# Seven block products in three of eight pairs of channel tiles, and SwiGLU transposes issued ten steps later

## The chip, the core and the metric

The kernel runs on one core of a Trainium2 chip, all by itself. The metric is the device time of one execution in microseconds (us). TensorE (PE) multiplies matrices, VectorE (DVE) and ScalarE (ACT) work element by element, SyncE (SP) issues the transfers (DMAs) that bring weights from the chip's memory into the core's. Every engine works through its own list of instructions in order; semaphores make one wait for another.

## What is computed

A decoder layer for 256 tokens of width 2048 in float32: a norm, one input projection, eight heads of differential attention and eight heads of gated DeltaNet, an output projection, and then the part that the change touches, a norm and a SwiGLU feed-forward block with 5632 hidden channels:

```python
    u = rmsnorm(h, ffn_norm_w[l])
    h = h + (jax.nn.silu(u @ w_gate[l]) * (u @ w_up[l])) @ w_down[l]
```

## The kernel before

Each weight element in float32 is used as the sum of two shorter numbers: `split` (lines 263 to 274) lets ScalarE round a raw weight tile to `hi` (L272) and VectorE take the rest, `lo = raw - hi` (L273). TensorE then computes three products for each block (hi by hi, hi by lo, lo by hi).

The feed-forward block works on chunks of 512 hidden channels; chunk 0 is done by `stream`, chunks 1 to 10 by `chunk` (L1369). In a chunk the 16 channel tiles of `u` (128 channels each) are taken as eight pairs q = 0 to 7, and for each pair a gate weight tile and an up weight tile of 128 x 1024 (512 KB) are loaded. An ordinary pair takes 2 x 2 blocks of tokens and channels for two outputs, 8 block products or 24 matmuls of 512 columns. In the pairs listed in `SEVEN` the same is done with seven block products (Strassen's scheme in Winograd's form), 21 matmuls. For that the weights are combined too: VectorE makes `t` (L290, L291: u1-g1 and u2-u1) and `s` (L296, L297: u2-t1 and g2-s1) from the raw gate tile g and up tile u, and g, half of u, t and s are each split. So an ordinary pair has two weight forms, and a pair of seven has four, called g, u, t and s.

The weights go through rings of buffers. Raw tiles have 4 buffers (`WR`): a load is issued when the tile four places before it has been read for the last time, an ordinary tile by L273, the u and g of a pair of seven by L296 and L297. `hi` and `lo` have 6 buffers: a form's split waits until TensorE is done with the form six places before.

A chunk gathers in four banks x0 to x3 of the matmuls' memory, gate in x0 and x1, up in x2 and x3, and what the seven products share in four other banks, y0 to y3. There are eight banks in all, and two rings of four that change roles from chunk to chunk: the y banks of one chunk are the x banks of the next. After the last pair of seven, `mid_task` (L1337) copies y0 (ScalarE, L1343) and adds up y1 to y3 (VectorE, L1345 to L1348), which frees these banks. After the gate half of pair 7, `end_task` (L1352) adds x0, x1 (L1357), applies SiLU, adds x2, x3 (L1362), multiplies (L1364), waits some steps and goes on in `to_hT` (L1272): TensorE transposes the 128 x 512 result in four pieces (L1277), ScalarE and VectorE copy it out as two parts (L1292, L1293). The transposes use two banks of the x ring of their chunk, which the next chunk needs as its y banks.

What sets the order: the tasks are Python generators, and `tasks.step()` is called after each block product (three matmuls). `yield 2` means that the task goes on two steps later. ScalarE and SyncE keep the order in which the code is written; TensorE and VectorE are ordered by a scheduler of the framework. The profile's names are `aux` and `mm` for the two rings of banks, `gact` for the tiles of `mid_task` and `end_task`, `raw`, `hi`, `lo`, `t` and `s` for the weights, `uh`, `ul`, `sh`, `sl` for the stationary operands.

Of the kernel before, what the change touches and what calls it, by code (L numbers as in the profile page):

```python
# [8 lines left out]
F32 = mybir.dt.float32  # L9
F32R = mybir.dt.float32r  # L10
# [5 lines left out]
P = 128  # L16
D = 2048
KT = D // P
META = 16
SEQ = 256  # L20
T = META + SEQ
FFN = 5632
H = 8
# [8 lines left out]
WR, WS = 4, 4  # L32
WS2 = 2
WHOLE = 8
SEVEN = (2, 5)
PER_STEP = 2
SLOT = 4
WARM = 14
# [127 lines left out]
def layer(tc, xT, aw, x, w_in, w_ba, w_out, w_gate, w_up, w_down, cmask, dist, par, out):  # L166
# [3 lines left out]
    def pool(name, bufs=1, space=None):  # L170
        cm = tc.tile_pool(name=name, bufs=bufs, **({"space": space} if space else {}))
        return cm, cm.__enter__()
# [7 lines left out]
    cm_const, const = pool("const")  # L180
# [6 lines left out]
    cm_work, wk = pool("work")  # L187
# [15 lines left out]
    def act(out_, in_, func, **kw):  # L203

        act_table("silu_and_others" if func == AF.Silu else "natural_log_exp_and_others")
        S.activation(out_, in_, func, **kw)

    def mark(k, n=1):
        done[k] = done.get(k, 0) + n

    def at_least(k, n):
        return lambda: done.get(k, 0) >= n
# [20 lines left out]
    def w_tile(wv, q, c):  # L233
        return wv[:, 2 * q:2 * q + 2, 512 * c:512 * (c + 1)], 2, 512
# [5 lines left out]
    for c in range(1, NCH):  # L240
        for q in range(KT // 2):
            i = len(order)
            order += [w_tile(wv, q, c) for wv in (wg_v, wu_v)]
            forms += [("w", i), ("w", i + 1)] if q not in SEVEN else [("g", i), ("u", i), ("t", i), ("s", i)]
    i = len(order)
# [95 lines left out]
    def mk(n):  # L341
        return cmsk[:, CMI[n] - 1, :]
# [15 lines left out]
    def small(n):  # L358
        smalls[0] += 1
        return const.tile([P, 17], F32, tag="small", bufs=6, name=f"small{smalls[0]}")[:, 0:n]  # L360
# [33 lines left out]
            square((k - 6) // 2)  # L394


    rbc = const.tile([P, T], F32, name="rbc")

    def input_rms():

# [151 lines left out]


    qkv = {n: None for n in "qkv"}
    blk64 = const.tile([P, P], F32R, name="blk64r")
    V.tensor_copy(blk64, mk("blk64"))
    tri_s = const.tile([P, P], F32R, name="tri_sr")
    V.tensor_copy(tri_s, mk("tri_s"))
    cwv = pr("conv_w").rearrange("p (c j) -> p c j", j=4)

# [33 lines left out]
    c2 = const.tile([P, 17], F32, name="c2")  # L594
    rq = const.tile([P, 16], F32, name="rq")
    rq2 = const.tile([P, 16], F32, name="rq2")
    kP = const.tile([P, H, META], F32, name="kP")
    kPf = kP.rearrange("p h t -> p (h t)")

    ktm = {}  # L600

    def sums(which, g, n, dst, keep_it=False):

        ps = yield from aux.get(4, P)
        for i in range(4):
            PE.transpose(ps[:, i, :], qkv[which][:, 4 * g + i, META + P * n:META + P * (n + 1)], ident)
        yield 1
        junk = yield from r1.get(P)
        for i in range(4):
            c = 8 * n + 4 * g + i  # L610
            S.activation(junk, ps[:, i, :], AF.Square, accum_out=dst[:, c:c + 1])
        r1.free()
        if keep_it:
            ktm[g] = yield from r2.get(4, P)
            V.tensor_copy(ktm[g], ps)
        aux.free()

    def k_scalars():
        yield at_least("gates", 1)
        ssk = const.tile([P, 17], F32, name="ssk")  # L620
        for g in range(2):
            yield at_least(f"k{g}", 4)
            yield 3
            for n in range(2):
                yield from sums("k", g, n, ssk, n == 0)
        G.tensor_copy(kP, qkv["k"][:, :, 0:META])
        yield 2
        ps = yield from aux.get(P)
        PE.transpose(ps, kPf, ident)
        yield 1  # L630
        ktm["m"] = const.tile([P, P], F32, name="ktm_m")
        S.activation(ktm["m"], ps, AF.Square, accum_out=ssk[:, 16:17])
        S.copy(ktm["m"], ps)
        aux.free()
        yield 1
        rk, a = small(17), small(17)
        rsqrt_fine(rk, ssk, 1.0, a)
        V.tensor_tensor(ksq, a, rk, ALU.mult)
        V.tensor_tensor(c1, rk, rk, ALU.mult)
        V.tensor_tensor(c1, c1, gb, ALU.mult)  # L640
        V.tensor_tensor(c2, c1, e_rem, ALU.mult)
        mark("c1")
# [709 lines left out]
    def end_task(c, b, x, t):  # L1352
        ring = rings[c % 2]
        yield at_least(f"mid{c}", 1)
        g_, h_ = t[2 * b], t[2 * b + 1]
        r_ = rr[:, b:b + 1]
        V.tensor_tensor(g_, x[b], g_, ALU.add)  # L1357
        ring.free()
        act(g_, g_, AF.Silu, scale=r_)
        yield at_least(f"up{c}", 1)  # L1360
        yield 1
        V.tensor_tensor(h_, x[2 + b], h_, ALU.add)  # L1362
        ring.free()
        V.scalar_tensor_tensor(h_, h_, r_, g_, ALU.mult, ALU.mult)  # L1364
        fpool[1].free()
        yield 2
        yield from to_hT(c, b, h_)

    def chunk(c):  # L1369
# [3 lines left out]
        y, t = [], []  # L1373
        n = KT // 2 - len(SEVEN)
        left = {("x", i): 3 * (2 * n + (len(SEVEN) if i < 3 else 0)) for i in range(4)}
        left.update({("y", i): 3 * len(SEVEN) for i in range(4)})
        todo = dict(left)
# [6 lines left out]
        for q in range(KT // 2):  # L1384
            k = 2 * q
            if q not in SEVEN:
                for col in range(2):
# [16 lines left out]
            for part in plan:  # L1404
                hi, lo = next_w()
                for bank, a, i in part:
                    product(bank, a, (hi[:, i], lo[:, i]))
                    tasks.step()
            if q == SEVEN[-1]:
                tasks.spawn(mid_task(c, y, t), urgent=True)  # L1410
# [146 lines left out]
```

## Time and profile before

| | |
|---|---|
| time, median of 3 runs | 1244.05 us (1243.71 to 1245.04) |
| profiled execution, its own time | 1242.6 us |
| its span, first to last instruction | 1240.8 us |
| TensorE busy | 1228.4 us, 99% |
| VectorE busy | 865.0 us, 70% |
| ScalarE busy | 652.2 us, 53% |
| DMA queue of SyncE | 226.78 MB, 56.6% of 16 engines' span |

Matmuls are pipelined, and the view shows each of them with its latency, 0.39 us, while the next starts 0.23 us after it; a busy TensorE is therefore read by the distance between starts. Inside the span the feed-forward chunks 1 to 10 lie between 558 and 995 us, and the down projection from there to the end. 1.8 us of the profiled execution lie outside its span.

### The profile page before, as it was taken

What the parts mean: (1) busy time and instruction counts of PE and PEld (TensorE: products, weight loads), DVE (VectorE), ACT (ScalarE), POOL (GpSimd) and SP (SyncE); (2) the same over time, 40 slices, a digit from 0 to 9 for tenths busy, and PEclk for the clock granted to TensorE, in tenths of its full rate; (3) what the DMA queues carried; (4) which work ended last, traced back from release to release, by engine and by line L of the source; (5) the groups of instructions that cost most, each with busy time, mean ns of one, the idle gap of its engine ahead of it and who ended that gap; (6) DMA issues with size and microseconds to landing.
All of it is one profiled execution on the core that took longest, in us unless ns stands there. A gap on an engine that the chain in (4) does not pass through costs nothing.

```text
span 1240.8 us, 19041 instructions
## 1 busy us (share of the span) xinstructions
PE 1228.4 (99%) x7388; PEld 1072.9 (86%) x7388; DVE 865.0 (70%) x1357; ACT 652.2 (53%) x1021; POOL 6.0 (0%) x14
## 2 busy tenths in 40 slices
PE   9999999999999999999999999999999999999998
PEld 7999999999999888888888888888888878888887
DVE  7989965686677655667887887788787764444442
ACT  7675465375676654555555555455555553433331
POOL 0000000000000000000000000000000000000000
PEclk9999999999999999999999999999999999999999
DMA  8466553345544555675566656456565675656561
GB/s 292 125 199 194 166 171 120 107 136 153 154 143 147 204 187 183 234 235 163 188 202 200 194 183 219 159 195 207 190 195 190 208 259 195 207 198 206 193 215 52
DMA packets 151003, 228.53 MB, mean 184 GB/s; under 512 B 11640, under 2 KB 72576, under 8 KB 150144
## 3 DMA queue, kind: packets, MB, share of 16 engines
q1 hardware_dynamic: 150368, 226.78, 56.6%
q8 instruction: 58, 0.95, 0.3%
q10 hardware_dynamic: 544, 0.52, 0.1%
q14 instruction: 33, 0.27, 0.1%
HBM read 221.83 MB, written 5.45 MB: 183 GB/s over the span
## 4 chain that ended last, share of the span: by engine, by line
PE 77%; DVE 12%; DMA 4%; ACT 4%; issue 2%; SPq 0%; ACTq 0%; DVEq 0%
PE mm L1152 22%; PE mm L1199 19%; PE aux L1382 10%; PE mm L1382 9%; PE aux L1199 9%; DVE lo L273 6%; ACT hi L272 3%; DMA raw<-in_w_gate_dram 2%; DMA raw<-in_w_up_dram 1%; DVE gact L1357 1%; DVE gact L1362 1%; PE aux L1100 1%; DVE gact L1364 1%; PE aux L1277 1%; PE aux L1055 1%
## 5 line engine op out<-in xcount | busy, mean ns | idle before, releaser
L273 DVE TENSOR_TENSOR lo<-raw,hi 128x1024 fp32r<-128x1024 f32 (+1 forms) x412 | 484.2, 1186 | 291.9 <-ACT hi L272 288.4
L272 ACT CAST hi<-raw 128x1024 fp32r<-128x1024 f32 (+1 forms) x412 | 417.6, 1022 | 428.7 <-PE mm L1199 114.0
L1152 PE MATMUL mm<-xh,hi 128*128 128x272 f32 (+2 forms) x896 | 258.3, 289 | 0.0
L1152 PE MATMUL mm<-xl,hi 128*128 128x272 f32 (+2 forms) x896 | 255.7, 286 | 0.6 <-DVE xl L384 0.6
L1152 PE MATMUL mm<-xh,lo 128*128 128x272 f32 (+2 forms) x896 | 254.9, 285 | 0.8 <-DVE lo L273 0.8
L1152 PEld LDWEIGHTS mm<-xh,hi 128*128 128x128 f32 x896 | 168.7, 189 | 2.1 <-issue 1.5
L1152 PEld LDWEIGHTS mm<-xl,hi 128*128 128x128 f32 x896 | 168.5, 188 | 1.8 <-DVE xl L384 1.5
L1152 PEld LDWEIGHTS mm<-xh,lo 128*128 128x128 f32 x896 | 168.2, 188 | 1.1 <-DVE lo L273 1.0
L1382 PE MATMUL aux<-hi,uh 128*128 128x512 f32 x280 | 109.4, 391 | 0.0
L1382 PE MATMUL mm<-hi,uh 128*128 128x512 f32 x280 | 109.4, 391 | 0.0
L1382 PE MATMUL aux<-hi,ul 128*128 128x512 f32 x280 | 109.3, 390 | 0.0
L1382 PE MATMUL mm<-hi,ul 128*128 128x512 f32 x280 | 109.0, 389 | 0.0
L1382 PE MATMUL aux<-lo,uh 128*128 128x512 f32 x280 | 108.9, 389 | 0.0
L1382 PE MATMUL mm<-lo,uh 128*128 128x512 f32 x280 | 108.9, 389 | 0.0
L1199 PE MATMUL aux<-hi,hT 128*128 128x512 f32 x256 | 79.7, 390 | 0.0
L1199 PE MATMUL mm<-hi,hT 128*128 128x512 f32 x256 | 79.2, 389 | 0.0
L1382 PEld LDWEIGHTS mm<-hi,ul 128*128 128x128 f32 x280 | 52.6, 188 | 11.1
L1382 PEld LDWEIGHTS aux<-hi,ul 128*128 128x128 f32 x280 | 52.6, 188 | 10.8
L1382 PEld LDWEIGHTS aux<-lo,uh 128*128 128x128 f32 x280 | 52.6, 188 | 10.8
L1382 PEld LDWEIGHTS mm<-lo,uh 128*128 128x128 f32 x280 | 52.6, 188 | 10.8
L1382 PEld LDWEIGHTS aux<-hi,uh 128*128 128x128 f32 x280 | 52.6, 188 | 10.8
L1382 PEld LDWEIGHTS mm<-hi,uh 128*128 128x128 f32 x280 | 52.6, 188 | 10.7
(395 smaller groups left out, 1753.0 us busy)
## 6 DMA issues: line engine op xcount, KB each, us to landing
raw<-in_w_in_dram SPq DMA_DIRECT2D x111, 512.0 KB, 3.6
raw<-in_w_gate_dram SPq DMA_DIRECT2D x88, 512.0 KB, 4.2
raw<-in_w_up_dram SPq DMA_DIRECT2D x88, 512.0 KB, 4.5
raw<-in_w_down_dram SPq DMA_DIRECT2D x88, 512.0 KB, 4.4
raw<-in_w_out_dram SPq DMA_DIRECT2D x32, 512.0 KB, 4.1
x1n<-x1d SPq DMA_DIRECT2D x2, 1024.0 KB, 7.7
xr<-in_xT_dram SPq DMA_DIRECT2D x7, 272.0 KB, 5.6
out_dram<-x1n SPq DMA_DIRECT2D x6, 256.0 KB, 5.6
```

Source lines behind the costliest of these rows:

```text
L272: S.copy(hi[:, js], raw[:, js])
L273: V.tensor_tensor(lo[:, js], raw[:, js], hi[:, js], ALU.subtract)
L1055: PE.matmul(pss[m][:, cut[n]], q[ms, P * n:P * (n + 1)], k[ms, 0:NK[n]], start=True, stop=True)
L1100: PE.matmul(po[:, n, :], l, r, start=(j == 0), stop=(j == 1 + n))
L1152: PE.matmul(acc[c][:, 0:n], a[:, k, cs], b[:, kt, t0:T], start=(kt == 0 and i == 0), stop=(kt == KT - 1 and i == 2))
L1199: PE.matmul(acc[b], l, r[:, i % 2, :], start=(first and i == 0 and j == 0), stop=(last and i == len(kts) - 1 and j == 2))
L1277: PE.transpose(pst[:, j, :], h_[:, P * j:P * (j + 1)], ident)
L1357: V.tensor_tensor(g_, x[b], g_, ALU.add)
L1362: V.tensor_tensor(h_, x[2 + b], h_, ALU.add)
L1364: V.scalar_tensor_tensor(h_, h_, r_, g_, ALU.mult, ALU.mult)
L1382: PE.matmul((x if bank[0] == "x" else y)[bank[1]], l, r, start=first, stop=todo[bank] == 0)
```

## The change

`SEVEN` becomes (2, 4, 6): three pairs of seven in a chunk in place of two, and the last of them is pair 6 in place of 5, so that `mid_task` is spawned one pair later. In `end_task` ten steps, in place of two, lie between L1364 and the transposes. Five small tiles move from a pool that lives to the end to one that is closed before the feed-forward block, which makes room for the side operands of the third pair.

```diff
-SEVEN = (2, 5)
+SEVEN = (2, 4, 6)
...
-    rbc = const.tile([P, T], F32, name="rbc")
+    rbc = wk.tile([P, T], F32, name="rbc")
...
         ring.free()
         V.scalar_tensor_tensor(h_, h_, r_, g_, ALU.mult, ALU.mult)
         fpool[1].free()
-        yield 2
+        yield 10
         yield from to_hT(c, b, h_)
```

The tiles `blk64r`, `tri_sr`, `kP` and `ktm_m` move like `rbc`. L-numbers of the changed kernel are the same, since no line is added.

VectorE from the last pair of seven on, before (pairs 5 to 7; raw_8987 and raw_8975 are u and g of pair 5):

```order
L290 TENSOR_TENSOR t_9014<-raw_8987,raw_8975 128x512
L291 TENSOR_TENSOR t_9014<-raw_8987 128x512
L273 TENSOR_TENSOR lo_9018<-raw_8987,hi_9017 128x512
L296 TENSOR_TENSOR s_9033<-raw_8987,t_9014 128x512
L297 TENSOR_TENSOR s_9033<-raw_8975,s_9033 128x512
L273 TENSOR_TENSOR lo_9037<-t_9014,hi_9036 128x1024
L273 TENSOR_TENSOR lo_9057<-s_9033,hi_9056 128x1024
L273 TENSOR_TENSOR lo_9073<-raw_8996,hi_9072 128x1024
```

VectorE in the same place now, from the end of pair 4 to the end of pair 6 (raw_9119 and raw_9091 are u and g of pair 6, raw_8983 is g of pair 4):

```order
L297 TENSOR_TENSOR s_9082<-raw_8983,s_9082 128x512
L273 TENSOR_TENSOR lo_9100<-s_9082,hi_9099 128x1024
L273 TENSOR_TENSOR lo_9116<-raw_9054,hi_9115 128x1024
L290 TENSOR_TENSOR t_9152<-raw_9119,raw_9091 128x512
L273 TENSOR_TENSOR lo_9134<-raw_9089,hi_9133 128x1024
L273 TENSOR_TENSOR lo_9146<-raw_9091,hi_9145 128x1024
L291 TENSOR_TENSOR t_9152<-raw_9119 128x512
L273 TENSOR_TENSOR lo_9156<-raw_9119,hi_9155 128x512
L296 TENSOR_TENSOR s_9165<-raw_9119,t_9152 128x512
L273 TENSOR_TENSOR lo_9169<-t_9152,hi_9168 128x1024
L297 TENSOR_TENSOR s_9165<-raw_9091,s_9165 128x512
L273 TENSOR_TENSOR lo_9183<-s_9165,hi_9182 128x1024
```

The first instruction on the new up tile (L290) now stands ahead of two splits of tiles that were loaded before it, and the split of s stands directly behind L297, with no other split between them.

VectorE from `mid_task` on, before (the `lo` rows are the splits of pairs 1 and 2 of the next chunk; x banks here are aux, y banks mm):

```order
L1345 TENSOR_TENSOR gact_9145<-mm_8968,gact_9144 128x512
L273 TENSOR_TENSOR lo_9163<-raw_9115,hi_9162 128x1024
L1346 TENSOR_TENSOR gact_9146<-mm_8969,gact_9145 128x512
L1347 TENSOR_TENSOR gact_9147<-mm_8970,gact_9146 128x512
L1348 TENSOR_TENSOR gact_9145<-mm_8970,gact_9145 128x512
L273 TENSOR_TENSOR lo_9181<-raw_9127,hi_9180 128x1024
L1357 TENSOR_TENSOR gact_9144<-aux_8868,gact_9144 128x512
L1357 TENSOR_TENSOR gact_9146<-aux_8869,gact_9146 128x512
L273 TENSOR_TENSOR lo_9199<-raw_9139,hi_9198 128x1024
```

VectorE from `mid_task` on, now (lo_9262 is the last split of pair 1 of the next chunk, lo_9289 the first of its pair 2):

```order
L273 TENSOR_TENSOR lo_9262<-raw_9232,hi_9261 128x1024
L1345 TENSOR_TENSOR gact_9271<-mm_9047,gact_9270 128x512
L273 TENSOR_TENSOR lo_9289<-raw_9241,hi_9288 128x1024
L1346 TENSOR_TENSOR gact_9272<-mm_9048,gact_9271 128x512
L1357 TENSOR_TENSOR gact_9270<-aux_8947,gact_9270 128x512
L1347 TENSOR_TENSOR gact_9273<-mm_9049,gact_9272 128x512
L1348 TENSOR_TENSOR gact_9271<-mm_9049,gact_9271 128x512
L1357 TENSOR_TENSOR gact_9272<-aux_8948,gact_9272 128x512
```

`mid_task` now stands behind all splits of pairs 0 and 1 of the next chunk and around the first split of its pair 2; before, the two splits of pair 1 stood in and behind it.

TensorE at the transposes, before (gact_8795 and gact_8797 are the two results of the chunk before; hi_8785 and lo_8786 are the up tile of pair 0):

```order
L1382 MATMUL aux_8871<-lo_8786,uh 128x512
L1277 MATMUL mm_8895<-ident,gact_8795 128x128 x4
L1382 MATMUL aux_8871<-hi_8785,ul 128x512
L1277 MATMUL mm_8900<-ident,gact_8797 128x128 x4
L1382 MATMUL aux_8870<-hi_8785,uh 128x512
```

TensorE at the transposes, now (hi_8888 and hi_8900 are the gate and the up tile of pair 1):

```order
L1382 MATMUL aux_8948<-lo_8889,uh 128x512
L1382 MATMUL aux_8948<-hi_8888,ul 128x512
L1277 MATMUL mm_9013<-ident,gact_8910 128x128 x4
L1277 MATMUL mm_9018<-ident,gact_8912 128x128 x4
L1382 MATMUL aux_8949<-hi_8900,uh 128x512
```

The transposes move from the middle of pair 0 to the middle of pair 1 (in every other chunk, where the rings have changed roles, to three matmuls before its end).

## Rows read from the trace of the kernel before

**Rows 1.** The page: busy time of each engine over the whole span (part 1), and the chain that ended last, its shares by engine (part 4).

```profile
PE 1228.4 (99%) x7388; PEld 1072.9 (86%) x7388; DVE 865.0 (70%) x1357; ACT 652.2 (53%) x1021; POOL 6.0 (0%) x14
...
PE 77%; DVE 12%; DMA 4%; ACT 4%; issue 2%; SPq 0%; ACTq 0%; DVEq 0%
```

**Rows 2.** The chain of waits in order of time, in the feed-forward part: start us, us, what. Each of the three 6.84 us pieces is the first stretch of matmuls behind the transposes of a chunk: of the second chunk, of the third, and of the tenth.

```profile
607.93 6.84 PE mm L1382 x30
...
618.85 11.56 PE mm L1382 x51
...
651.51 6.84 PE aux L1382 x30
...
956.66 6.84 PE mm L1382 x30
```

**Rows 3.** Busy time by stretch, one chunk each: stretch, its us, then us (and count) of PE, PEld, DVE, ACT, POOL, then the granted TensorE clock (1.00 is the upper level, 2.4 GHz), the DMA share and GB/s.

```profile
607.90:651.50 43.60, 43.31 (x196) 35.64 (x195) 34.97 (x41) 23.00 (x25) 0.00 (x0) 1.00 0.59 193
```

**Rows 4.** TensorE in order of time at the start of the third chunk: start us, us, engine, line, operation, tiles, shape, and in brackets the idle time before it and what ended it. The transposes are the rows of L1277.

```profile
649.51 0.39 PE L1382 MATMUL aux<-lo,uh 128*128 128x512 f32 x1
650.18 0.66 PE L1277 MATMUL mm<-ident,gact 128*128 128x128 f32 x4 [0.28 <-DVE gact L1364]
650.60 0.48 PE L1382 MATMUL aux<-hi,ul 128*128 128x512 f32 x1
650.91 0.60 PE L1277 MATMUL mm<-ident,gact 128*128 128x128 f32 x4
651.27 0.48 PE L1382 MATMUL aux<-hi,uh 128*128 128x512 f32 x1
651.58 0.39 PE L1382 MATMUL aux<-lo,uh 128*128 128x512 f32 x1
```

**Rows 5.** The same view behind the last chunk (its transposes stand between matmuls of the down projection).

```profile
998.35 0.66 PE L1277 MATMUL mm<-ident,gact 128*128 128x128 f32 x4 [0.84 <-DVE gact L1364]
...
1000.15 0.66 PE L1277 MATMUL mm<-ident,gact 128*128 128x128 f32 x4 [0.45 <-DVE gact L1364]
```

**Rows 6.** VectorE in order of time around the start of the third chunk (columns as in rows 4; "x2" is two instructions merged).

```profile
642.33 0.68 DVE L1348 TENSOR_TENSOR gact<-aux,gact 128x512 f32<-128x512 f32 x1
642.92 1.21 DVE L273 TENSOR_TENSOR lo<-raw,hi 128x1024 fp32r<-128x1024 f32 x1
644.06 1.28 DVE L1357 TENSOR_TENSOR gact<-mm,gact 128x512 f32<-128x512 f32 x2
...
646.39 0.69 DVE L290 TENSOR_TENSOR t<-raw,raw 128x512 f32<-128x512 f32 x1
...
647.59 0.68 DVE L273 TENSOR_TENSOR lo<-raw,hi 128x512 fp32r<-128x512 f32 x1
648.19 1.28 DVE L1362 TENSOR_TENSOR gact<-mm,gact 128x512 f32<-128x512 f32 x2
649.39 1.40 DVE L1364 SCALAR_TENSOR_TENSOR gact<-gact,rr,gact 128x512 f32<-128x512 f32 x2
...
651.31 1.22 DVE L273 TENSOR_TENSOR lo<-t,hi 128x1024 fp32r<-128x1024 f32 x1
652.45 0.68 DVE L297 TENSOR_TENSOR s<-raw,s 128x512 f32<-128x512 f32 x1
653.05 1.28 DVE L1293 TENSOR_TENSOR hT<-mm,hT 128x512 fp32r<-128x512 f32 x2
654.33 1.23 DVE L273 TENSOR_TENSOR lo<-s,hi 128x1024 fp32r<-128x1024 f32 x1
```

**Rows 7.** ScalarE in order of time, same stretch.

```profile
631.85 3.05 ACT L272 CAST hi<-raw 128x1024 fp32r<-128x1024 f32 x3 [0.31 <-PE mm L1382]
636.55 1.05 ACT L272 CAST hi<-raw 128x1024 fp32r<-128x1024 f32 x1 [1.65 <-DMA raw<-in_w_up_dram]
...
653.24 1.05 ACT L272 CAST hi<-s 128x1024 fp32r<-128x1024 f32 x1 [1.11 <-DVE s L297]
```

**Rows 8.** The DMA queue of SyncE in order of time: issues of weight loads.

```profile
607.89 0.37 SPq L259 DMA_DIRECT2D raw<-in_w_gate_dram  x1
609.59 0.37 SPq L259 DMA_DIRECT2D raw<-in_w_up_dram  x1
...
653.16 0.37 SPq L259 DMA_DIRECT2D raw<-in_w_up_dram  x1
```

**Rows 9.** Weight loads, us from issue to landing: minimum, median and maximum of those issued between 620 and 650 us.

```profile
DMA to landing us min/median/max: 3.5/4.3/5.5
```

**Rows 10.** The same for single loads, by the view of DMA issues over a window that holds one issue (last column: us to landing): the one issued at 607.89 us, the one at 609.59 us, the one at 641.11 us and the one at 636.46 us.

```profile
raw<-in_w_gate_dram SPq DMA_DIRECT2D x1, 512.0 KB, 3.5
...
raw<-in_w_up_dram SPq DMA_DIRECT2D x1, 512.0 KB, 4.4
...
raw<-in_w_gate_dram SPq DMA_DIRECT2D x1, 512.0 KB, 3.6
...
raw<-in_w_gate_dram SPq DMA_DIRECT2D x1, 512.0 KB, 5.2
```

**Rows 11.** VectorE while the first chunk starts: two instructions of the helper that builds the side operands.

```profile
556.35 0.55 DVE L1332 TENSOR_TENSOR sl<-gact,sh 128x384 fp32r<-128x384 f32 x1
...
557.42 0.28 DVE L1321 TENSOR_TENSOR gact<-gact 128x128 f32<-128x128 f32 x1
```

**Rows 12.** TensorE at the transposes that follow the first column block, in the first chunk.

```profile
562.10 0.66 PE L1277 MATMUL mm<-ident,gact 128*128 128x128 f32 x4 [0.67 <-DVE gact L1306]
```

More of the change, by code (lines that the diff above doesn't have):

```diff
@@ L554, in layer @@
     qkv = {n: None for n in "qkv"}
-    blk64 = const.tile([P, P], F32R, name="blk64r")
+    blk64 = wk.tile([P, P], F32R, name="blk64r")
     V.tensor_copy(blk64, mk("blk64"))
-    tri_s = const.tile([P, P], F32R, name="tri_sr")
+    tri_s = wk.tile([P, P], F32R, name="tri_sr")
     V.tensor_copy(tri_s, mk("tri_s"))
@@ L596, in layer @@
     rq2 = const.tile([P, 16], F32, name="rq2")
-    kP = const.tile([P, H, META], F32, name="kP")
+    kP = wk.tile([P, H, META], F32, name="kP")
     kPf = kP.rearrange("p h t -> p (h t)")
@@ L630, in k_scalars @@
         yield 1
-        ktm["m"] = const.tile([P, P], F32, name="ktm_m")
+        ktm["m"] = wk.tile([P, P], F32, name="ktm_m")
         S.activation(ktm["m"], ps, AF.Square, accum_out=ssk[:, 16:17])
```

## The prediction, made before the changed kernel was run

> **What bounds the kernel now.** I read the page first. TensorE is busy for 99% of the span, VectorE for 70%, and the chain that ended last is TensorE for 77% and VectorE for 12% [rows 1]. Then I read the feed-forward part, which alone is changed, in the chain in order of time [rows 2]: 51 matmuls take 11.56 us there, 0.2267 us each, and from the second chunk to the tenth one period is (956.66 - 607.93) / 8 = 43.59 us. A chunk has six ordinary pairs of 24 matmuls and two pairs of seven with 21, 186 in all, which makes 42.16 us. What is left, 1.43 us, lies at the transposes: after the matmul at 649.51 the next could start 0.23 us later, but the transposes start at 650.18 and wait for L1364, which costs 0.44 us; the other 1.0 us is the eight transposes themselves [rows 4]. So the chunks are bound by TensorE, with one short wait for VectorE. Last I read VectorE in the same stretch: 34.97 us busy of 43.60 [rows 3]. It has 8.6 us to spare on the average, and the question is whether these lie where the change needs them.
>
> **The change: what goes.** A third pair of seven saves 3 matmuls in each of ten chunks: 30 x 0.2267 = 6.8 us. The transposes, eight steps (24 matmuls, 5.4 us) later, no longer meet an L1364 that is 0.44 us late: 9 x 0.44 us, and behind the last chunk 0.84 + 0.45 us [rows 5], together 5.3 us. A chunk could then take 43.59 - 0.68 - 0.44 = 42.47 us, and the kernel 12.1 us less.
>
> **What comes, once.** The third set of side operands (seven VectorE instructions, one like the halves below, five of 0.2 us by their distance and one of 0.5, [rows 11], 2.1 us) stands partly ahead of the results that the first transposes already wait 0.67 us for [rows 12]. Between nothing and 2.1 us I take 0.5 us, since half of the set stands behind. Its ScalarE casts have their cover, as ScalarE waits most of the time [rows 7].
>
> **What comes in each chunk.** VectorE's work, by distances between starts in [rows 6]: a full split 1.14 us (651.31 to 652.45), an operation of half that size 0.60 us (652.45 to 653.05), the two L1364 together 1.3 us. A chunk now has 10 full splits of ordinary pairs and 3 x 3 of pairs of seven, 19 x 1.14 = 21.7 us; 25 of the half size (five in each pair of seven, four in `mid_task`, six in both `end_task`s), 15.0 us; with L1364 38.0 us. That is 4.1 us more than before, as a pair of seven takes 3 x 1.14 + 5 x 0.60 = 6.4 us and an ordinary one 2.3 us. That alone would fit into 42.47 us. But VectorE takes its instructions in order, and the new order holds waits that no other work fills. I follow one round from the start of L297 of pair 6 (time 0) to the same in the next chunk, as if TensorE never held it up.
>
> - The split of s needs its cast first. From L297 to that split it takes 652.45 to 654.33, 1.88 us, where 0.60 us would be the distance [rows 6, 7]. Before, other work stood between; in pairs 4 and 6 none does now: 2 x 1.28 = 2.6 us. Three shorter gaps of this kind add 0.3 us.
> - L290 of pair 6 needs the up tile of that pair, whose load waits for L297 of pair 4: the queue issues 0.03 us behind its end (653.16, [rows 8]), 0.71 us after its start. VectorE has two splits left meanwhile, to 1.88 + 2 x 1.14 = 4.16 us. With the median landing of 4.3 us [rows 9] L290 starts at 5.05: 0.9 us idle. Behind it stand the splits of 5u and 6g, for which TensorE has 2 us of lead and more.
> - The gate tile of the next pair 1 is loaded when the split of 7g is over: 1.88 + 1.14 + 1.23 = 4.25 us. Its issue stands alone, 3.6 us behind the one before, like the one at 641.11 that landed in 3.6 us [rows 10]; it lands at 7.9, the cast takes 1.05 us [rows 7] and some 0.1 us of gaps, and its split starts at 9.0, where VectorE would have been at 7.6: 1.4 us. The up tile is issued 1.14 us later; at 4.3 us it adds 0.7 us.
>
> The round is 38.0 + 2.6 + 0.3 + 0.9 + 1.4 + 0.7 = 43.9 us. These load waits are in no trace of before, where TensorE set the pace; a round grows by 2 us for each us of landing (once at L290, once at pair 1). If all land in 3.5 us (the shortest, [rows 9]) it is 42.3 us and hidden under 42.47; if all take 5.2 us, as in a burst [rows 10], 45.7 us. I take 43.9, by the median, because the loads of the round are spaced neither as widely as the fastest nor as densely as the slowest.
>
> **Who pays for it.** Before, L1348, which frees the last y bank, is over at 642.33 + 0.68 = 643.0 [rows 6]. The next chunk starts 16 matmuls before 649.51, at 645.9 [rows 4], and first writes that bank (as x3) 15 matmuls, 3.4 us, later: 6.3 us of cushion. The change spawns `mid_task` one pair later, 24 matmuls or 5.4 us, so 0.9 us are left before VectorE is any later at all. The first chunk and the change to the second have that cushion; at the eight changes into chunks 3 to 10 TensorE waits in front of its x banks for the excess of the round, 43.9 - 42.47 = 1.4 us. That is 8 x 1.43 = 11.5 us. So the wait of 0.44 us at the transposes would come back, three times as long, at the start of the chunk.
>
> **The sum.** -6.8 - 5.3 + 0.5 + 11.5 = -0.1 us. The profiled execution took 1242.6 us, 1.8 us of it outside its span of 1240.8, and lies 1.45 us below the median of the runs, 1244.05. So 1242.5 for such an execution, and 1244.0 us for the median: no difference that can be told. What a measurement of this kernel can tell from no change is about 0.2%, 2.5 us.
>
> **Rival 1: VectorE keeps up.** The waits for loads are shorter than I put them, TensorE stays the bound, and most of the 11.6 us are kept: 1232.4 us with landings of 3.5 us, 1237.7 us with 3.9 (round 43.1 us). For it: lone loads land in 3.5 and 3.6 us [rows 10], and a round that is starved issues its loads more evenly. Against it: the load at 609.59, 1.7 us behind another, took 4.4 us, and that is just the spacing of the two loads of pair 6 [rows 8, 10]. The Trainium skill speaks for this rival ("DMA: Bandwidth & Descriptors", section "Anatomy of one DMA"): it fits a transfer, for the queue of another engine, as about 2.0 us plus its bytes at 436 GB/s, an estimate of 3.2 us for 512 KB. By it the round would be some 41.7 us and the change worth its full 11.6 us; no load in these rows is that fast. I give this rival 0.33.
>
> **Rival 2: the loads are late (slower).** One mechanism at one place: the raw tiles of a pair of seven keep their buffers until L296 and L297, and with three such pairs a load is issued so late that VectorE waits for it, at L290 of pair 6 and at pair 1. It decides from a landing of about 4.5 us on, where the round passes 44.2 us and the sum 2.5 us. With 4.7 us it is 44.7 us, 8 x 2.2 = 18 us given back and 1250 us; with the 5.2 us of the burst 45.7 us and 1258 us. For it: the two loads of [rows 10] that follow another closely took 4.4 and 5.2 us, and half of all take 4.3 us or more [rows 9]. Against it: in a burst the issues follow one another by 1.1 us, here mostly by more. Chance 0.31.
>
> **Rival 3: the change does not do all it says.** The transposes now stand shortly before pair 2, whose third part writes the two banks that they used. Nine matmuls, 2.0 us, lie between, and L1293 has to follow ScalarE's cast by then. If it is 0.6 us late in every other chunk, 3 us of the gain are lost: 1235.4 us where VectorE else keeps up, nothing where TensorE already waits. It lies within the first rival.
>
> **How the numbers follow.** No difference 0.36, with the forecast 1244.0 us and its own range of 1241.5 to 1246.5; faster 0.33; slower 0.31. The range of 1237 to 1251 us is that of landings from 3.9 to 4.7 us and leaves out a tenth on either side.
>
> **What would show it.** Matmuls of L1382: 30 fewer. At the transposes no wait for L1364 of more than 0.1 us in most chunks. A wait of TensorE of 1 to 2 us at the first matmuls of chunks 3 to 10, ended by L1345 to L1348; chunk periods of 43.5 to 44.3 us, VectorE busy for some 39 of them. VectorE idle for about 1 us before L290 of pair 6 with a DMA as its releaser, 1.3 us twice before the split of s. I am wrong if the periods are near 42.5 us (the loop is not closed, or the loads are faster), if they are over 44.5, or if TensorE waits elsewhere, for `hi` or `lo` of a pair of seven.

## The result, and the profile after

The changed kernel took 1247.1 us in the median of its runs (1244.0 to 1252.5), the kernel before 1243.9 us beside it; the ratio is 1.0026, with a 95% interval of 1.0017 to 1.0035. That is 2.1 to 4.4 us slower: little, but the interval leaves out no change. The forecast was 1244.0 us, no difference; 1247.1 lies inside the range of 1237 to 1251 us, but outside the 1241.5 to 1246.5 us that the forecast gave to no difference. (One run of 1452 us, at a mean granted clock of 0.78, is left out of the comparison.) The profiled execution took 1246.6 us, with a span of 1244.8 us against 1240.8 before.

The page of the changed kernel, busy time (part 1) and the chain by engine (part 4), as in [rows 1]:

```profile
PE 1225.3 (98%) x7358; PEld 1066.3 (86%) x7358; DVE 905.0 (73%) x1424; ACT 661.6 (53%) x1043; POOL 6.0 (0%) x14
...
PE 62%; DVE 20%; DMA 9%; issue 5%; ACT 4%; SPq 0%; ACTq 0%; DVEq 0%
```

TensorE has its 30 matmuls less, and VectorE 40 us more of work. TensorE's share of the chain fell from 77 to 62%; VectorE and the DMAs, which had 16% together, have 29%. To see the chunks alone I cut the trace at a fixed point of VectorE's work, the last multiply of `mid_task` (L1348): between the first of these and the ninth lie eight whole rounds. Busy time by stretch over them, columns as in [rows 3]:

```profile
604.10:959.90 355.80, 346.92 (x1535) 280.57 (x1533) 307.93 (x367) 190.08 (x217) 0.00 (x0) 1.00 0.59 189
```

355.8 / 8 = 44.48 us per chunk. TensorE alone would need 42.47 us, so 8 x 2.0 = 16 us are given back, where the forecast had 11.5. VectorE is busy for 307.9 / 8 = 38.5 us of a round and idle for 6.0. What TensorE waited for in this stretch (engine, operation's output and line, what it waited for, us in total, times, longest us):

```profile
PE aux L1382 <- DVE gact L1348: 2.4, 4, 0.8
PE mm L1382 <- DVE gact L1348: 1.7, 3, 0.7
PE mm L1382 <- ACT gact L1343: 1.4, 2, 0.7
PE aux L1382 <- DVE gact L1345: 1.3, 4, 0.4
PE mm L1382 <- DVE gact L1345: 1.2, 3, 0.4
PE aux L1382 <- ACT gact L1343: 0.7, 1, 0.7
```

These are the banks that the first matmuls of a chunk write, and `mid_task` has to leave them first. The waits at the transposes [rows 4] are gone, and nothing waits for L1293. The rows add up to 8.7 us, not 16, and the busy time holds the rest: eight rounds of a later experiment (4), with the same matmuls, have 340.5 us of busy TensorE, not 346.9. One of these waits, in order of time:

```profile
692.68 0.39 PE L1382 MATMUL mm<-hi,ul 128*128 128x512 f32 x1
693.77 0.50 PE L1382 MATMUL mm<-hi,uh 128*128 128x512 f32 x1 [0.70 <-DVE gact L1348]
694.11 0.39 PE L1382 MATMUL mm<-lo,uh 128*128 128x512 f32 x1
```

Listed are 0.70 us, but from start to start it takes 1.09 us in place of 0.23, and the next matmul again 0.34. Read so, the 17 waits cost 13.4 us and not 8.7. The period is the sum to trust. And VectorE's idle time in the same eight rounds, by group (busy us, mean ns | idle us before, and what ended it):

```profile
L273 DVE TENSOR_TENSOR lo<-raw,hi 128x1024 fp32r<-128x1024 f32 x104 | 123.7, 1220 | 21.2 <-ACT hi L272 21.1
L273 DVE TENSOR_TENSOR lo<-s,hi 128x1024 fp32r<-128x1024 f32 x24 | 29.4, 1226 | 18.5 <-ACT hi L272 17.9
L273 DVE TENSOR_TENSOR lo<-t,hi 128x1024 fp32r<-128x1024 f32 x24 | 29.3, 1222 | 0.0
L290 DVE TENSOR_TENSOR t<-raw,raw 128x512 f32<-128x512 f32 x24 | 16.5, 687 | 8.2 <-DMA raw<-in_w_up_dram 8.2
```

So no wait of VectorE ends with TensorE; it waits for loads, and for casts. One round of it in order of time, pair 4's split of s first, with the rows between left out where they have no wait:

```profile
667.86 1.23 DVE L273 TENSOR_TENSOR lo<-s,hi 128x1024 fp32r<-128x1024 f32 x1 [1.19 <-ACT hi L272]
...
670.78 0.69 DVE L290 TENSOR_TENSOR t<-raw,raw 128x512 f32<-128x512 f32 x1 [0.56 <-DMA raw<-in_w_up_dram]
...
676.69 0.68 DVE L297 TENSOR_TENSOR s<-raw,s 128x512 f32<-128x512 f32 x1
678.57 1.23 DVE L273 TENSOR_TENSOR lo<-s,hi 128x1024 fp32r<-128x1024 f32 x1 [1.20 <-ACT hi L272]
...
683.50 1.23 DVE L273 TENSOR_TENSOR lo<-raw,hi 128x1024 fp32r<-128x1024 f32 x1 [0.29 <-ACT hi L272]
685.79 1.23 DVE L273 TENSOR_TENSOR lo<-raw,hi 128x1024 fp32r<-128x1024 f32 x1 [1.06 <-ACT hi L272]
688.17 1.23 DVE L273 TENSOR_TENSOR lo<-raw,hi 128x1024 fp32r<-128x1024 f32 x1 [1.16 <-ACT hi L272]
```

Every wait of the forecast is there, in its place: the split of s behind L297 in pairs 4 and 6, L290 of pair 6 behind a load, and the two splits of the next pair 1 (685.79 the gate tile, 688.17 the up tile). The last two name the cast, and the cast itself waits for the load. The queue's issues at that place:

```profile
680.96 0.37 SPq L259 DMA_DIRECT2D raw<-in_w_gate_dram  x1
682.10 0.37 SPq L259 DMA_DIRECT2D raw<-in_w_up_dram  x1
683.23 0.37 SPq L259 DMA_DIRECT2D raw<-in_w_gate_dram  x1
684.75 0.37 SPq L259 DMA_DIRECT2D raw<-in_w_up_dram  x1
```

The gate tile of pair 1 was issued at 680.96 and landed in 3.6 us, as forecast. The up tile, at 682.10, is the second of four issues 1.1 to 1.5 us apart; the two behind it landed in 5.7 and 5.5 us. For the up tile itself the profile has no landing here, and its cast, at 687.09, is listed behind VectorE's split of the gate tile, which ended 0.07 us before and of which the cast reads nothing. In four of the seven rounds with this order the cast is listed behind the load itself; the issue and the cast of one of them:

```profile
770.94 0.37 SPq L259 DMA_DIRECT2D raw<-in_w_up_dram  x1
...
776.36 1.05 ACT L272 CAST hi<-raw 128x1024 fp32r<-128x1024 f32 x1 [1.90 <-DMA raw<-in_w_up_dram]
```

A cast starts 0.1 us after the landing that it waits for, so the up tile took 5.3 us there, 4.5 to 5.3 in the four rounds, and some 4.9 in the one above. The forecast had 4.3.

### The profile page after: what moved, and what is told of

The parts are those of the page before. It is cut to its first block, busy times and chain, and to the rows that moved or that the text cites. A ratio compares the mean times of both kernels' runs of the same rounds, so it can differ in the third digit from the quotient of the medians.

```text
span 1244.8 us, 19089 instructions
## 1 busy us (share of the span) xinstructions
PE 1225.3 (98%) x7358; PEld 1066.3 (86%) x7358; DVE 905.0 (73%) x1424; ACT 661.6 (53%) x1043; POOL 6.0 (0%) x14
## 4 chain that ended last, share of the span: by engine, by line
PE 62%; DVE 20%; DMA 9%; issue 5%; ACT 4%; SPq 0%; ACTq 0%; DVEq 0%
PE mm L1152 22%; PE mm L1199 19%; DVE lo L273 11%; PE aux L1199 10%; DMA raw<-in_w_up_dram 6%; ACT hi L272 3%; PE aux L1382 3%; DMA raw<-in_w_gate_dram 2%; DVE t L291 1%; DVE s L297 1%; DVE s L296 1%; PE mm L1382 1%; PE aux L1100 1%; DVE t L290 1%; DVE gact L1364 1%
## 5 line engine op out<-in xcount | busy, mean ns | idle before, releaser
L273 DVE TENSOR_TENSOR lo<-raw,hi 128x1024 fp32r<-128x1024 f32 (+1 forms) x412 | 477.7, 1172 | 239.0 <-ACT hi L272 236.7
L272 ACT CAST hi<-raw 128x1024 fp32r<-128x1024 f32 (+1 forms) x412 | 410.6, 1010 | 340.5 <-PE mm L1199 112.3
L1382 PE MATMUL mm<-hi,uh 128*128 128x512 f32 x260 | 102.8, 396 | 4.9 <-DVE gact L1348 2.2
L1382 PE MATMUL aux<-hi,uh 128*128 128x512 f32 x260 | 102.9, 396 | 4.4 <-DVE gact L1348 2.4
L1382 PE MATMUL aux<-hi,ul 128*128 128x512 f32 x260 | 101.4, 390 | 0.0
L1382 PE MATMUL aux<-lo,uh 128*128 128x512 f32 x260 | 101.3, 390 | 0.0
L1382 PE MATMUL mm<-hi,ul 128*128 128x512 f32 x260 | 101.3, 390 | 0.0
L1382 PE MATMUL mm<-lo,uh 128*128 128x512 f32 x260 | 101.3, 389 | 0.0
L272 ACT CAST hi<-s 128x1024 fp32r<-128x1024 f32 x30 | 31.6, 1052 | 73.3 <-DVE s L297 56.3
L1382 PEld LDWEIGHTS mm<-hi,uh 128*128 128x128 f32 x260 | 48.8, 188 | 18.9 <-DVE gact L1348 3.9
L1382 PEld LDWEIGHTS aux<-hi,uh 128*128 128x128 f32 x260 | 48.8, 188 | 18.5 <-DVE gact L1348 4.1
L1382 PEld LDWEIGHTS mm<-hi,ul 128*128 128x128 f32 x260 | 48.8, 188 | 10.3
L1382 PEld LDWEIGHTS aux<-hi,ul 128*128 128x128 f32 x260 | 48.8, 188 | 10.3
L1199 PEld LDWEIGHTS aux<-hi,hT 128*128 128x128 f32 x256 | 48.0, 188 | 10.7 <-DVE gact L1345 0.6
```

The source lines that it names most:

```text
L272: S.copy(hi[:, js], raw[:, js])
L273: V.tensor_tensor(lo[:, js], raw[:, js], hi[:, js], ALU.subtract)
L1199: PE.matmul(acc[b], l, r[:, i % 2, :], start=(first and i == 0 and j == 0), stop=(last and i == len(kts) - 1 and j == 2))
L1382: PE.matmul((x if bank[0] == "x" else y)[bank[1]], l, r, start=first, stop=todo[bank] == 0)
```

## The experiments

The theory: VectorE takes its instructions in order, and its own round (work, and waits for casts and loads that nothing fills) is longer than TensorE's 42.47 us, so it sets the chunk. The rivals are that TensorE's side sets it, that the later transposes cost something at their banks, and that only one of the two kinds of wait counts. All times are ratios to the kernel before, run beside them (its median was 1245.0 to 1245.9 us there). Period, busy and idle time are of VectorE over eight rounds between L1348 and L1348, as above, divided by eight (where a run adds lines, the same instruction a few lines lower).

| run | us | ratio (95%) | period | busy | idle |
|---|---|---|---|---|---|
| before, first trace | 1243.9 | 1 | 43.59 | 34.7 | 8.9 |
| after, first trace | 1247.1 | 1.0026 (1.0017 to 1.0035) | 44.48 | 38.5 | 6.0 |
| 1 two pairs, late transposes | 1236.0 | 0.9924 (0.9910 to 0.9939) | 43.04 | 34.7 | 8.4 |
| 2 three pairs, early transposes | 1255.2 | 1.0074 (1.0056 to 1.0092) | 45.00 | 38.6 | 6.4 |
| 3 two splits left out | 1233.3 | 0.9903 (0.9886 to 0.9920) | 42.65 | 36.4 | 6.2 |
| 4 VectorE's order fixed | 1231.3 | 0.9886 (0.9869 to 0.9903) | 42.59 | 39.2 | 3.4 |
| 5 after, again | 1248.5 | 1.0023 (1.0012 to 1.0033) | 44.78 | 38.5 | 6.3 |
| 6 order fixed, s uncovered | 1254.9 | 1.0075 (1.0058 to 1.0092) | 45.35 | 38.9 | 6.5 |
| 7 order fixed, two pairs | 1235.6 | 0.9919 (0.9905 to 0.9932) | 43.10 | 35.3 | 7.8 |
| 8 two more load buffers | 1230.4 | 0.9873 (0.9857 to 0.9890) | 42.46 | 38.5 | 3.9 |
| 9 more buffers, two pairs | 1235.3 | 0.9924 (0.9912 to 0.9937) | 43.08 | 34.6 | 8.5 |
| 10 order fixed, more buffers | 1228.5 | 0.9871 (0.9856 to 0.9886) | 42.39 | 39.0 | 3.4 |
| 11 four pairs | 1256.5 | 1.0092 (1.0078 to 1.0105) | 45.43 | 43.1 | 2.3 |
| 12 before, again | 1246.1 | 0.9995 (0.9983 to 1.0007) | 43.78 | 34.8 | 9.0 |

A period comes from one execution. Those of runs 5 and 6 were the longest of their runs, 3.3 and 4.2 us above the median, and that of run 9 was the longest too, by some 2 us.

**1: the second edit alone.**

```diff
-SEVEN = (2, 4, 6)
+SEVEN = (2, 5)
```

> The second edit alone: two pairs of seven per chunk (third and sixth) as before, transposes issued ten steps later. Theory (VectorE's in-order round, with its waits for casts and loads, sets the chunk once there are three pairs of seven): the round here is that of before, well under TensorE's 43.15 us, so only the transposes' wait goes: 9 x 0.44 and 1.3 us behind the last chunk, about 5 us, 1238 to 1239.5 us. Rival (issuing the transposes ten steps later costs elsewhere, at the banks that pair 2 writes, and that is where the changed kernel lost its gain): 1243 us or more, with waits of TensorE on L1293 or L1306 in every chunk.

The period is 43.04 us, TensorE's floor with two pairs, and TensorE's waits list nothing between 601 and 1000 us. So the later transposes cost nothing at their banks. The gain of 7.6 to 11.2 us is more than the 5 us expected (12 comes back to that).

**2: the first edit alone.**

```diff
-        yield 10
+        yield 2
         yield from to_hT(c, b, h_)
```

> The first edit alone: three pairs of seven, transposes two steps after the gate as before. Theory: VectorE's round stays 44.5 us and sets the chunk; where TensorE spends its spare 2 us, at the x banks or at the transposes, makes no difference: 1246 to 1248.5 us, the waits at the transposes back (0.4 to 2 us per chunk) and those at the x banks shorter by as much. Rival (TensorE's own work sets the chunk, and the two edits add up): 1243.9 - 6.8 + 0.5 = 1237.6 us, since only the transposes' wait would be left.

Slower than either: TensorE waits in the chunks at the x banks and at the transposes too, 0.5 to 0.7 us each. I had expected the changed kernel's time; by the ratios it is some 6 us longer. Its span is 1253.4 us, 8.6 over the first trace of the changed kernel (1244.8). Of that 4.2 us lie in the eight rounds, and 4.2 in the ninth and behind it, where the changed kernel has only 0.2 us of waits (TensorE's waits from 1000 us on):

```profile
PE mm L1277 <- DVE gact L1364: 1.4, 1, 1.4
PE aux L1199 <- ACT gact L1343: 1.3, 1, 1.3
PE aux L1199 <- DVE gact L1345: 0.4, 1, 0.4
```

Why the rounds are longer, 45.00 us in place of 44.48 (44.78 in the fifth run), I can't put down to one place; so where TensorE waits does make a difference, and the theory does not say why. The rival, 1237.6 us, is out.

**3: two of VectorE's splits left out.** The helper gives back `(hi, hi)` for the gate and up tiles of pair 3.

```diff
+    SKIP = set()
...
+            SKIP.update((len(forms), len(forms) + 1) if q == 3 else ())
...
-            V.tensor_tensor(lo[:, js], raw[:, js], hi[:, js], ALU.subtract)
-        return hi, lo
+            if n not in SKIP:
+                V.tensor_tensor(lo[:, js], raw[:, js], hi[:, js], ALU.subtract)
+        return (hi, hi) if n in SKIP else (hi, lo)
```

> The changed kernel, with the remainders of the gate and up tiles of the pair of index 3 not computed and the rounded parts used in their place: the output is then not the reference's; matmuls, loads and casts are all there, and VectorE has two splits of 1.14 us less in each chunk. Theory: the round goes from 44.5 to 42.2 us, under TensorE's 42.47, and nearly all that was given back returns: 1231 to 1235 us. Rival 1 (the wait for loads alone is what counts, and the loads come no earlier): the splits taken away become idle time in front of the next load, 1244 to 1247 us. Rival 2 (TensorE's side sets the chunk): no change, 1247 us.

2.3 us of VectorE's work per chunk bring the period to 42.65 us, and the time 12 us below the kernel before, with every matmul, load and cast of the changed kernel still there. TensorE's side does not set the chunk of the changed kernel; VectorE's round does. How much of the gain is the work alone this run can't tell: two load buffers per chunk now come free with the cast, and not with the split behind it, so two loads are issued earlier too.

**4: the order of VectorE fixed.** In the changed kernel a scheduler orders VectorE; here it follows the text of the program during the chunks.

```diff
+    cm_order.__exit__(None, None, None)
+    cm_order = tc.manual_schedule(engines=PINNED | {ET.DVE})
+    cm_order.__enter__()
     for c in range(1, NCH):
         chunk(c)
...
```

> The changed kernel with VectorE held to the order of the program text during the chunks; the same instructions, but L296 and L297 come ahead of the split of t, so the split of s no longer stands right behind the cast it needs (1.28 us, twice per chunk), and L290 of pair 6 stands behind the splits of 5u and 6g (0.6 us of waiting for its load). Theory: the round loses up to 2 x 1.28 + 0.6 = 3.2 us and falls to 41.3 us, under TensorE's 42.47: 1231 to 1236 us. Rival 1 (the waits at the loads of the next pair 1 swallow what is gained, since the loads move with the round): 1240 to 1245 us. Rival 2 (TensorE's side sets the chunk): no change, 1247 us.

The same instructions in another order take the kernel from 1.0026 to 0.9886 of the kernel before. TensorE's order stays: the 1918 matmuls and transposes of the chunks (L1382, L1277) follow one another by name as in the changed kernel, but for six records. The end of pair 6, where the split of t now stands between L297 and the split of s:

```profile
672.73 0.69 DVE L297 TENSOR_TENSOR s<-raw,s 128x512 f32<-128x512 f32 x1
673.34 1.22 DVE L273 TENSOR_TENSOR lo<-t,hi 128x1024 fp32r<-128x1024 f32 x1
674.62 1.23 DVE L273 TENSOR_TENSOR lo<-s,hi 128x1024 fp32r<-128x1024 f32 x1
```

The groups of VectorE in the eight rounds:

```profile
L273 DVE TENSOR_TENSOR lo<-raw,hi 128x1024 fp32r<-128x1024 f32 x104 | 124.9, 1221 | 22.5 <-ACT hi L272 20.7
L273 DVE TENSOR_TENSOR lo<-s,hi 128x1024 fp32r<-128x1024 f32 x24 | 29.4, 1225 | 1.5
...
L290 DVE TENSOR_TENSOR t<-raw,raw 128x512 f32<-128x512 f32 x24 | 16.4, 684 | 0.0
```

18.5 us before the split of s have become 1.5, and 8.2 us before L290 nothing. What stays stands mostly at the next pair 1 and is hidden: TensorE waits 0.2 us in all.

**5: the changed kernel once more**, without an edit.

> The changed kernel itself, unedited, so that it stands beside the kernel before and the other experiments on one chip. Theory: as when it was first timed, 1.0017 to 1.0035 of the kernel before, rounds of 44.4 to 44.6 us; if the single loads land 0.2 us later on this chip than in the first trace (3.6 to 3.7 us in place of 3.4 to 3.5), the round is up to 0.4 us longer, and the time up to 3 us. Rival (the round does not depend on the landing): the same time whatever the loads take.

The ratio agrees with the first measurement. Over the whole kernel the gate loads took 4.0 us in the median in place of 3.6, the up loads 4.6 in place of 4.4, and the round is 0.30 us longer. Nearly all of that is L290's wait for its load, 10.4 us in place of 8.2; the waits before the split of s did not move:

```profile
L273 DVE TENSOR_TENSOR lo<-s,hi 128x1024 fp32r<-128x1024 f32 x24 | 29.4, 1225 | 18.4 <-ACT hi L272 17.9
...
L290 DVE TENSOR_TENSOR t<-raw,raw 128x512 f32<-128x512 f32 x24 | 16.4, 685 | 10.4 <-DMA raw<-in_w_up_dram 10.4
```

**6: one of the two waits put back** into the fourth.

```diff
-                V.tensor_tensor(s[:, 1], g[:, 1], s[:, 0], ALU.subtract)
-                pos[3] += 2
                 ready[m] = split(t, m, a, b)
+                V.tensor_tensor(s[:, 1], g[:, 1], s[:, 0], ALU.subtract)
+                pos[3] += 2
```

> The kernel with VectorE's order fixed, with one thing put back as the scheduler had it: L297 stands behind the split of t, so the split of s follows it directly and has to wait for its cast, in all three pairs of seven. Theory: VectorE's free round under the fixed order is some 41 us (38.5 of work and up to 2.6 of waiting at the next pair 1), and 3 x 1.2 us come back: 44.7 us, 43.5 if pair 2 still has cover; above TensorE's 42.5 us either way: 1240 to 1251 us. Rival 1 (the wait of L290 in pair 6 for its load was what cost the changed kernel its gain, and that wait stays away here): 1231 to 1235 us. Rival 2 (waits of this kind are taken from the later waits at pair 1, so they add nothing): 1231 to 1235 us too, but then with the idle time before the split of s there and that at pair 1 gone.

One instruction that changes places with a split costs 23 us:

```profile
L273 DVE TENSOR_TENSOR lo<-raw,hi 128x1024 fp32r<-128x1024 f32 x104 | 123.1, 1219 | 21.1 <-ACT hi L272 20.8
L273 DVE TENSOR_TENSOR lo<-s,hi 128x1024 fp32r<-128x1024 f32 x24 | 29.4, 1225 | 28.7 <-ACT hi L272 28.7
```

The wait before the split of s is back, 24 times 1.2 us, and that at pair 1 is as long as in the fourth run: it was not taken from there, it is added. The period, 45.35 us, is 0.65 us above what I had worked out, since the fixed order has more work per round than the 38.5 us that I took from the changed kernel (38.9 busy, and short gaps besides). L290 does not wait here at all, so the split of s is enough by itself to make VectorE the bound. TensorE's listed waits end here mostly with ScalarE's copy of y0 (L1343, 12.7 of 14.9 us), which stands in ScalarE's list behind the cast of the up tile of pair 1.

**7: the fixed order with two pairs.**

```diff
-SEVEN = (2, 4, 6)
+SEVEN = (2, 5)
```

> Two pairs of seven, transposes ten steps later, and VectorE's order fixed: the first experiment with the order fixed. Theory: TensorE sets the chunk in both, so fixing the order brings nothing here: 1235 to 1237.5 us, like the first experiment, and 4 to 7 us above the fixed order with three pairs (30 matmuls of 0.2267 us, less what the third set of side operands costs). Rival (the fixed order is a gain by itself, in some other place): clearly below 1235 us, as far below the first experiment as the fixed order was below the changed kernel.

As expected: the fixed order is worth nothing where VectorE has time to spare. Between the seventh and the fourth, the third pair of seven is worth 4 us.

**8: loads two tiles earlier.** A second pool of two load buffers, and one extra buffer for split tiles in place of two, so that it fits.

```diff
-WS2 = 2
+WS2 = 1
+WR2 = 2
...
+            if more and pos[0] % (WR + WR2) >= WR:
+                raw = more[0].tile([P, a, b], F32, tag="raw2", bufs=WR2, name=f"raw{pos[0]}")
...
-        load_to(pos[3] + WR - 1)
+        load_to(pos[3] + WR - 1 + (WR2 if more else 0))
```

> The changed kernel with six buffers for loaded tiles in place of four, and five for split tiles in place of six (so that they fit): loads are issued two tiles earlier. Theory: the waits for loads (1.0 us before L290 and up to 2.6 us at the next pair 1, per round) go for the most part, the waits before the split of s (2.2 us) stay: a round of 41 to 43 us, TensorE's 42.5 us decides: 1231 to 1240 us. Rival (only the order of VectorE counts, and idle time moves from the loads to the casts): 1244 us or more. A smaller reserve of split tiles may cost TensorE something by itself, which would show as waits of L1382 for lo or hi.

The period is TensorE's, 42.46 us. The groups (lines four higher here: L277 is the split, L294 was L290):

```profile
L277 DVE TENSOR_TENSOR lo<-raw,hi 128x1024 fp32r<-128x1024 f32 x104 | 122.2, 1218 | 13.0 <-ACT hi L276 12.0
L277 DVE TENSOR_TENSOR lo<-s,hi 128x1024 fp32r<-128x1024 f32 x24 | 29.4, 1223 | 4.6 <-ACT hi L276 4.5
...
L294 DVE TENSOR_TENSOR t<-raw,raw 128x512 f32<-128x512 f32 x24 | 16.5, 689 | 13.1 <-DMA raw<-in_w_up_dram 13.1
```

The wait before the split of s fell as well, which I had not expected: with other buffers the scheduler orders VectorE differently, and in all three pairs puts other work between L297 (L301 here) and that split. So this run does not separate the two kinds of wait; it shows that both can go without an order by hand. The loads themselves did not get faster, as the landing in the eight rounds shows (minimum, median, maximum; the first trace of the changed kernel, then this one; the fifth run, timed beside this one, has a median of 4.2):

```profile
DMA to landing us min/median/max: 3.3/4.0/6.0
```

```profile
DMA to landing us min/median/max: 3.5/4.6/6.2
```

**9: more buffers with two pairs**, the control to the eighth: its kernel with `SEVEN = (2, 5)`.

> Two pairs of seven, transposes ten steps later, and the six load buffers with five for split tiles: the control to the eighth experiment. Theory: TensorE's 43.15 us set the chunk with two pairs whatever the buffers, so the earlier loads bring nothing: 1235 to 1237.5 us, like the first experiment and the seventh. Rival (earlier loads are a gain by themselves, in the chunks or after them): 1231 to 1234 us.

The same ratio as the first run: the buffers alone bring nothing.

**10: both remedies**, the edits of the fourth and the eighth.

> Three pairs of seven with both remedies, VectorE's order fixed and six load buffers. Theory: the chunk is at TensorE's 42.47 us with either remedy, so both together bring next to nothing more: 1229.5 to 1231.5 us, chunk periods of 42.45 to 42.55 us. Rival (the two take away different waits of TensorE and add up): below 1228 us.

0.9871 against 0.9873 with buffers alone and 0.9886 with the order alone: the intervals cover each other, so they do not add up. With 1228.5 us, 14 to 18 us below the kernel before, it has the lowest median of all, but can't be told from the eighth.

**11: a fourth pair of seven**, with the order fixed, `WR2 = 1` and `WS2 = 1`.

```diff
-SEVEN = (2, 4, 6)
+SEVEN = (2, 4, 5, 6)
```

> A fourth pair of seven (indices 2, 4, 5 and 6), VectorE's order fixed, five load buffers and five for split tiles. TensorE's floor falls to 42.47 - 0.68 = 41.79 us. Theory: VectorE's work alone decides now, whatever the loads do: 39.2 us under the fixed order with three pairs, plus 3 x 1.14 + 5 x 0.60 - 2 x 1.14 = 4.1 us, 43.3 us per round, and up to 2.6 us of waits at the next pair 1: 8 x 1.5 us to 8 x 4 us above a floor of some 1224.5 us, 1236 to 1257 us; slower than three pairs. Rival (only waits for loads and casts held the changed kernel, and with them gone TensorE sets the chunk): 1224 to 1227 us.

The busy time by stretch over its eight rounds, and the first of TensorE's waits from 556 to 1000 us:

```profile
603.00:966.40 363.40, 346.17 (x1506) 272.34 (x1505) 344.70 (x415) 198.72 (x232) 0.00 (x0) 1.00 0.57 186
```

```profile
PE mm L1386 <- ACT hi L276: 8.8, 9, 1.2
PE aux L1386 <- ACT hi L276: 8.2, 9, 1.2
```

VectorE is busy for 344.7 / 8 = 43.1 us, beyond TensorE's 41.8, so the fourth pair's 30 matmuls buy nothing: it is 28 us slower than three pairs with the order fixed and six load buffers (10; here there are five, and what that one buffer costs is not separated). TensorE now waits for the casts of split tiles. The period, 45.4 us, is 2.3 us more than VectorE's work; this part I did not follow further.

**12: the kernel before once more**, without an edit.

> The kernel before, unedited, traced once more, because the second edit alone gained 7.6 to 11.2 us by the times, and 6.7 us from one trace to the other. Theory (the first trace of the kernel before caught an execution with short waits at the transposes; the usual wait is longer, as it hangs on when VectorE reaches L1364): chunk periods of 43.7 to 43.95 us in place of 43.59, with waits of TensorE for L1364 of 3 to 6 us in the chunks, a span of 1242 to 1244 us. Rival (the trace is typical, and the difference lies outside the chunks): a period of 43.5 to 43.65 us and a span of 1240 to 1241.5 us.

Its waits of TensorE from 556 to 1010 us:

```profile
PE mm L1277 <- DVE gact L1364: 2.4, 6, 0.5
PE aux L1277 <- DVE gact L1364: 2.2, 5, 0.6
```

4.6 us at the transposes, where the first trace has 2.7 in the same view, and a period of 43.78 us: the first trace of the kernel before caught an execution with short waits. The span, 1245.0 us, is longer than I expected, as 3.0 us were lost ahead of the first L1348 already (601.75 us in place of 598.75).

## Why the prediction was wrong, by its own steps

- **The bound and the mechanism were right.** With a third pair VectorE's in-order round, not its mean load, sets the chunk, and TensorE pays at the x banks of the next chunk (L1343, L1345, L1348). Shown by 4 (the same work in another order, nearly all comes back) and 6 (one wait put back, all is lost again), with 3 beside them, against the controls 1, 7 and 9.
- **VectorE's work, 38.0 us: right.** The busy time of 38.5 us counts an instruction ahead of a wait for its whole 1.22 us, where the forecast took the distance of 1.14. With 42 listed waits in eight rounds that is 0.08 us each, 0.4 us per round; without it the work is 38.1 us.
- **The waits, 5.9 us: 0.5 us too short, and this is the step that failed.** Counted as the forecast did, with that 0.08 us in each wait, they are 6.4 us. Split of s: 2.5 us (18.5 / 8, and two small shares) against 2.6, and of the 0.3 us of shorter gaps next to nothing is left. L290 of pair 6: 0.9, as forecast (the 8.2 us above hold 1.5 us at pair 4 too, in the last round). Gate tile of the next pair 1: waits of 1.06 to 1.40 us, 1.3 on the mean with the small share, against 1.4; the row that this was taken from, 641.11 [rows 10], itself stands only 2.2 us behind another load. Up tile of the next pair 1: 0.98 to 1.72 us, 1.4 on the mean with the small share, against 0.7. (Both in seven of the eight rounds; in the last the order there is another, with one wait of 2.3 us.) So the term that failed is "at 4.3 us it adds 0.7 us": it took the median landing for a load that is the second of four issues 1.1 to 1.5 us apart, and that landed in some 4.9 us. The forecast had put the issue 1.14 us behind the gate tile's, and it had the row of a load in such a burst, 5.2 us [rows 10], but used it for the far end of the range and the second rival only. That this load is late is read from the trace; no run made it alone land sooner.
- **From there to the sum.** A round of 44.48 us in place of 43.9 gives back 16 us in place of 11.5, so -0.1 becomes +4.4 us; between the two first traces it is 4.0, in the times 2.1 to 4.4. That the forecast missed by 3 us only is in part luck, as the next term was too small and works the other way: with the 6.7 us of the traces in its place the sum is 3.0.
- **The transposes' wait, 5.3 us: too small.** Alone, the edit gained 6.7 us between the traces and 7.6 to 11.2 in the times; part of that gap lies in the first trace of the kernel before, which had shorter waits than the second (12). That all of it comes from the transposes is not shown.
- **The third pair, 6.8 - 0.5 = 6.3 us:** 4.1 us by the ratios of 7 and 4, 6.6 by those of 9 and 10, where TensorE is the bound; each ratio is uncertain by some 2 us. About right.
- **The growth with the landing** ("2 us for each us") has the right sign: 0.30 us for a run in which gate loads took 0.4 us and up loads 0.2 us longer (5). The rule would give 0.4 to 0.8, half of it at pair 1, but almost all came at L290; so the size is not borne out.
- **The rivals.** The first (VectorE keeps up, loads in 3.5 to 3.9 us) fell on the landings; its time, 1232 us, is what 4 and 8 reach by other means. By the fit in the Trainium skill ("DMA: Bandwidth & Descriptors", section "Anatomy of one DMA"), which is for another queue, such a load would take an estimate of 3.2 us; the shortest in the rounds took 3.3 us and the median 4.0, and the measurement decides. The second came true at its low end: the round passed its 44.2 us and the kernel became slower. But only the up tile of pair 1 came late, not L290 of pair 6, and its prices, 1250 and 1258 us, were too high. The third did not happen.

## What to carry to other kernels

Where an engine takes its work in order, compare its whole round, waits included, with the bound engine's floor: 38.5 us of work would fit into 42.5, and the kernel still lost because 6 us of waits could not be filled. Look for an operation that stands directly behind the one that its cast depends on, and put independent work between; here moving one subtraction by one place, in each pair of seven, was worth 23 us. A load that is issued in a burst is to be priced by the loads of a burst in the trace, not by the median. Two more load buffers bought the waits off here, together with the other order that the scheduler then chose (8).

## What the runs showed of the hardware

- 512 KB loads of one queue mostly landed in 3.3 to 3.7 us when the issue before was 3.5 us back or more (the first trace of the changed kernel), and in 5.2 to 6.0 us as third or fourth of issues 1.1 to 1.5 us apart. With two more load buffers (8) the median was 4.6 us, where the changed kernel had 4.0 and 4.2, and the kernel was still shorter.
- A busy TensorE in the profile can be a waiting one: 346.9 us busy for the eight rounds of the changed kernel, 340.5 for the same rounds with VectorE's order fixed. The distance from start to start shows the wait in full: 1.09 us in place of 0.23, where 0.70 us are listed.
